# Two matmuls with a GELU between them: the loads, the start and the order of the first blocks rearranged

## The chip, the cores and the metric

One core of one Trainium2 chip. The metric is the device time of one execution in microseconds (us), the median of several executions. All times here are of undisturbed (fast) executions with a mean granted TensorE clock of 0.986 to 1.000 (the share of its full clock that the profile's records show). In the profile TensorE is PE (its weight loads PEld), ScalarE is ACT, VectorE is DVE, GpSimd is POOL and SyncE, which here issues loads and stores, is SP. "The span" is the stretch that the profile of one execution covers; the device time of that execution is some 1.7 us longer.

## The reference

```python
# x: 16 x 512 x 768, w1: 768 x 3072, b1: 3072, w2: 3072 x 768, all float32
y = np.matmul(x, w1) + b1
y = 0.5 * y * (1.0 + erf(y / np.sqrt(2.0)))
return np.matmul(y, w2).astype(np.float32)
```

The kernel works on 16 blocks of 512 rows. For each it computes layer 1 (x times w1, with GELU as y times sigmoid(1.702 y)) and layer 2 (times w2), in bf16 with float32 sums. Layer 1 goes through 24 output chunks of 128 columns (`hc` in the code), six matmuls each. The weights, 9.4 MB each, are loaded once, cast to bf16, and stay on the core.

## The kernel before

x arrives in rows and has to stand in columns, so each block is cast and turned by 24 transposes of 128x128 on TensorE, into PSUM and from there by copies into `xT`. A scheduler decides the order of the instructions on each engine from the order of the code and the times it assumes; only what stands under `manual_schedule` keeps the written order.

```python
w1st = ...tile_pool(name="w1st", bufs=12)     # 128 x 384 float32 each
w2st = ...tile_pool(name="w2st", bufs=4)      # 128 x 768
xfp  = ...tile_pool(name="xfp", bufs=4)       # 128 x 768
gtp  = ...tile_pool(name="gtp", bufs=1)       # layer 1's result of one block
ps_x = ...tile_pool(name="ps_x", bufs=1, space=PSUM)    # the transposes' only target

def stage_w1_group(g):                        # 384 of 3072 columns, six loads of 192 KB
    for kc in range(KC):
        w1s = w1st.tile([P, WG], FP32, name="w1s")
        nc.sync.dma_start(out=w1s[:], in_=w1[kc * P:(kc + 1) * P, c0:c0 + WG])
        # ... cast into w1b: DVE for even kc, ACT for odd

def stage_w2(hc):                             # 128 of 3072 rows, 384 KB, on ACT's DMA queue
    w2s = w2st.tile([P, N], FP32, name="w2s")
    nc.scalar.dma_start(out=w2s[:], in_=w2[hc * P:(hc + 1) * P, :])
    # ... cast into w2b: ACT for odd hc, DVE or GpSimd for even

xbfs0 = load_x_block(0, fast=True)            # four loads of 384 KB, a cast each
# ... bias load, identity
stage_w1_group(0)
xT_cur = transpose_x_block(xbfs0)             # 4 x 6 transposes through ps_x
for _g in range(1, NG):
    stage_w1_group(_g)
xbfs_next = load_x_block(1, fast=True)

for mb in range(n_mblk):
    gT = gtp.tile([P, HC, MB], BF16, name="gT")
    for hc in range(HC):                      # layer 1: 24 x 6 matmuls of 512 columns
        # ... matmuls of w1b and xT_cur into py; ACT: sig = sigmoid(1.702 py + b1s)
        # ... DVE: gT[:, hc, :] = (py + b1t) * sig
        if mb == 0:
            stage_w2(hc)
    if mb == 0:
        # ... layer 2 of block 0: three outputs side by side, in the order w2 arrives;
        # ... six transposes of block 1 after every sixth hc of the first half
    else:
        # ... layer 2: one output after another, 24 matmuls of 384 columns each;
        # ... six transposes of the next block after every second output
```

## Time and profile before

| | before |
|---|---|
| median of 16 runs | 1062.99 us (1060.54 to 1066.15) |
| span of the profiled run | 1058.8 us |
| TensorE busy | 97% |
| first big matmul | 20.70 us |
| first full layer 1 of block 1 begins | 102.42 us |
| one block in steady state | 63.62 us |

### The profile page before, as it was taken

What the parts mean: (1) busy time and instruction counts of PE and PEld (TensorE: products, weight loads), DVE (VectorE), ACT (ScalarE), POOL (GpSimd) and SP (SyncE); (2) the same over time, 40 slices, a digit from 0 to 9 for tenths busy, and PEclk for the clock granted to TensorE, in tenths of its full rate; (3) what the DMA queues carried; (4) which work ended last, traced back from release to release, by engine and by line L of the source; (5) the groups of instructions that cost most, each with busy time, mean ns of one, the idle gap of its engine ahead of it and who ended that gap; (6) DMA issues with size and microseconds to landing.
All of it is one profiled execution on the core that took longest, in us unless ns stands there. A gap on an engine that the chain in (4) does not pass through costs nothing.

```text
span 1058.8 us, 13724 instructions
## 1 busy us (share of the span) xinstructions
PE 1027.2 (97%) x5760; PEld 549.1 (52%) x5760; DVE 357.6 (34%) x527; ACT 355.7 (34%) x537; POOL 30.1 (3%) x41
## 2 busy tenths in 40 slices
PE   3789999999999999999999999999999999999998
PEld 1335464554645555465554645555465554645545
DVE  2531514325142341514325142341514315142340
ACT  4652513324142341513324142341513324142240
POOL 0021000000000000000000000000000000000000
PEclk9999999999999999999999999999999999999999
DMA  9974021120201102021120201102021010100001
GB/s 291 332 278 171 1 83 38 38 83 1 98 24 60 61 23 97 1 82 38 39 82 1 94 26 61 60 23 98 1 82 38 20 41 1 45 15 31 31 8 53
DMA packets 41167, 70.12 MB, mean 66 GB/s; under 512 B 7312, under 2 KB 29840, under 8 KB 41104
## 3 DMA queue, kind: packets, MB, share of 16 engines
q1 hardware_dynamic: 37648, 59.80, 16.8%
q10 hardware_dynamic: 3456, 9.44, 2.5%
q8 instruction: 45, 0.74, 0.3%
q14 instruction: 18, 0.15, 0.0%
HBM read 44.05 MB, written 25.17 MB: 65 GB/s over the span
## 4 chain that ended last, share of the span: by engine, by line
PE 92%; DMA 6%; SPq 1%; ACT 0%; DVE 0%; issue 0%; ACTq 0%
PE po L222 44%; PE py L147 44%; DMA w2s<-in_w_dram 3%; DMA w1s<-in_w_dram 2%; PE pxt L102 2%; PE po L196 1%; SPq L70 1%; PE po L209 1%; DMA xf<-in_x_dram 1%; ACT sig L155 0%; DVE gT L162 0%; ACT w1b L75 0%; ACT w2b L136 0%; DVE w1b L73 0%; DVE xbf L86 0%
## 5 line engine op out<-in xcount | busy, mean ns | idle before, releaser
L147 PE MATMUL py<-xT,w1b 128*128 128x512 bf16 x2304 | 506.3, 382 | 6.1 <-DVE gT L162 5.1
L222 PE MATMUL po<-w2b,gT 128*128 128x384 bf16 x2880 | 479.7, 326 | 0.0
L162 DVE SCALAR_TENSOR_TENSOR gT<-py,b1t,sig 128x512 bf16<-128x512 f32 x384 | 287.9, 751 | 294.9 <-ACT sig L155 294.9
L222 PEld LDWEIGHTS <-gT 128*128 128x128 bf16 x2880 | 279.2, 98 | 180.8
L147 PEld LDWEIGHTS <-w1b 128*128 128x128 bf16 x2304 | 226.1, 98 | 279.3 <-issue 10.4
L155 ACT ACTIVATE sig<-py,b1s 128x512 bf16<-128x512 f32 x384 | 263.1, 687 | 221.0 <-PE py L147 221.0
L182 DVE COPY osb<-po 128x384 f32<-128x384 f32 x64 | 35.5, 558 | 367.4 <-PE po L222 364.3
L184 ACT COPY osb<-po 128x384 f32<-128x384 f32 x64 | 30.4, 479 | 293.8 <-PE po L222 275.9
L108 ACT COPY xT<-pxt 128x768 bf16<-128x768 bf16 x32 | 25.5, 798 | 103.5 <-PE pxt L102 103.5
L102 PE MATMUL pxt<-ident,xbf 128*128 128x128 bf16 x384 | 33.2, 225 | 18.3 <-ACT xT L108 9.8
L95 POOL CAST xbf<-xf 128x768 bf16<-128x768 f32 x28 | 23.4, 838 | 760.2 <-PE pxt L102 756.1
L102 PEld LDWEIGHTS <-xbf 128*128 128x128 bf16 x384 | 27.5, 100 | 27.7 <-issue 10.9
L196 PE MATMUL po<-w2b,gT 128*128 128x384 bf16 x144 | 27.0, 330 | 3.7 <-ACT w2b L136 2.6
L93 ACT CAST xbf<-xf 128x768 bf16<-128x768 f32 x14 | 11.6, 831 | 45.1 <-PE pxt L102 45.1
L196 PEld LDWEIGHTS <-gT 128*128 128x128 bf16 x144 | 14.2, 99 | 14.8 <-issue 5.3
L110 DVE COPY xT<-pxt 128x768 bf16<-128x768 bf16 x32 | 17.6, 549 | 0.6 <-PE pxt L102 0.6
L75 ACT CAST w1b<-w1s 128x384 bf16<-128x384 f32 x24 | 12.3, 511 | 11.3 <-DMA w1s<-in_w_dram 11.2
L136 ACT CAST w2b<-w2s 128x768 bf16<-128x768 f32 x12 | 10.0, 830 | 14.4 <-DMA w2s<-in_w_dram 14.4
L73 DVE CAST w1b<-w1s 128x384 bf16<-128x384 f32 x24 | 8.6, 357 | 15.0 <-DMA w1s<-in_w_dram 15.0
L91 DVE CAST xbf<-xf 128x768 bf16<-128x768 f32 x14 | 8.1, 581 | 2.6 <-DMA xf<-in_x_dram 2.6
L209 PE MATMUL po<-w2b,gT 128*128 128x384 bf16 x48 | 8.3, 326 | 0.0
L134 POOL CAST w2b<-w2s 128x768 bf16<-128x768 f32 x7 | 6.0, 859 | 71.9 <-DMA w2s<-in_w_dram 71.9
(13 smaller groups left out, 16.7 us busy)
## 6 DMA issues: line engine op xcount, KB each, us to landing
xf<-in_x_dram SPq DMA_DIRECT2D x64, 384.0 KB, 3.2
out_dram<-osb SPq DMA_DIRECT2D x128, 192.0 KB, 1.9
w2s<-in_w_dram ACTq DMA_DIRECT2D x24, 384.0 KB, 5.3
w1s<-in_w_dram SPq DMA_DIRECT2D x48, 192.0 KB, 4.4
b1t<-in_b_dram SPq DMA_DIRECT2D x1, 12.0 KB, 7.6
```

The costliest lines, as they stand in the source:

```text
L95: nc.gpsimd.tensor_copy(out=xbf[:], in_=xf32[:])
L102: nc.tensor.transpose(out=pxt[:, kc, :], in_=xbfs[i][:, kc * P:(kc + 1) * P], identity=ident[:],)
L108: nc.scalar.copy(out=dst, in_=pxt[:, :, :])
L110: nc.vector.tensor_copy(out=dst, in_=pxt[:, :, :])
L147: nc.tensor.matmul(out=py[:], lhsT=w1b[:, kc, hc * P:(hc + 1) * P], rhs=xT_cur[:, kc, :], start=(kc == 0), stop=(kc == KC - 1),)
L155: nc.scalar.activation(out=sig[:], in_=py[:], func=mybir.ActivationFunctionType.Sigmoid, bias=b1s[:, hc:hc + 1], scale=1.702,)
L162: nc.vector.scalar_tensor_tensor(out=gT[:, hc, :], in0=py[:], scalar=b1t[:, hc:hc + 1], in1=sig[:], op0=mybir.AluOpType.add, op1=mybir.Alu ...
L182: nc.vector.tensor_copy(out=osb[:], in_=po[:])
L184: nc.scalar.copy(out=osb[:], in_=po[:])
L196: nc.tensor.matmul(out=pos[i][:], lhsT=gT[:, hc, i * P:(i + 1) * P], rhs=w2b[:, hc, nb * NB:(nb + 1) * NB], start=(hc == 0), stop=(hc == H ...
L209: nc.tensor.matmul(out=po3[:], lhsT=gT[:, hc, 3 * P:4 * P], rhs=w2b[:, hc, nb * NB:(nb + 1) * NB], start=(hc == 0), stop=(hc == HC - 1),)
L222: nc.tensor.matmul(out=po[:], lhsT=gT[:, hc, i * P:(i + 1) * P], rhs=w2b[:, hc, nb * NB:(nb + 1) * NB], start=(hc == 0), stop=(hc == HC - 1),)
```

## The change

Its intent: begin layer 1 sooner, leave the DMA to x and w1 first, and let w2 arrive behind layer 1 of two blocks. It has five parts: larger loads on one queue (SP's), three staging buffers for both weights; a start in fixed order with four PSUM targets for the transposes; layer 1 of blocks 0 and 1 before any layer 2 (which needs two `gT`); in steady state single transposes between the matmuls of layer 2; one store per 128 rows instead of two.

```diff
-    w1st = ctx.enter_context(tc.tile_pool(name="w1st", bufs=12))
-    w2st = ctx.enter_context(tc.tile_pool(name="w2st", bufs=4))
-    xfp = ctx.enter_context(tc.tile_pool(name="xfp", bufs=4))
+    wst = ctx.enter_context(tc.tile_pool(name="wst", bufs=3))
+    xfp = ctx.enter_context(tc.tile_pool(name="xfp", bufs=1))
-    gtp = ctx.enter_context(tc.tile_pool(name="gtp", bufs=1))
-    sigp = ctx.enter_context(tc.tile_pool(name="sigp", bufs=4))
+    gtp = ctx.enter_context(tc.tile_pool(name="gtp", bufs=2))
+    sigp = ctx.enter_context(tc.tile_pool(name="sigp", bufs=2))
 ...
+    def stage_w1_cols(c0, n):
+        w1s = wst.tile([P, KC, WG], FP32, name="ws")
+        nc.sync.dma_start(out=w1s[:, :, 0:n], in_=w1r[:, :, c0:c0 + n])
+        # ... six casts
+    def stage_w2_group(wg):
+        w2s = wst.tile([P, 3, N], FP32, name="ws")
+        nc.sync.dma_start(out=w2s[:], in_=w2r[:, 3 * wg:3 * wg + 3, :])
+        # ... three casts
 ...
+    with tc.manual_schedule(engines={PE, Activation, DVE, SP}):       # names shortened
+        xbfs0 = load_x_block(0, fast=True)
+        xT_cur = xtp.tile([P, KC, MB], BF16, name="xT")
+        for i in range(nsub):
+            pxt0 = (ps_o.tile(..., name="po") if i < 3 else ps_x.tile(..., name="pxt"))
+            for kc in range(KC):
+                transpose_x_kc(xbfs0, xT_cur, i, kc, pxt0)
+        stage_w1_cols(0, P)
+        stage_w1_cols(P, WG - P)
+        # ... bias load and b1s
     for _g in range(1, NG):
         stage_w1_group(_g)
     xbfs_next = load_x_block(1, fast=True)
 ...
-            if mb == 0:
-                stage_w2(hc)
+            if mb == 0 and hc % 3 == 0:
+                stage_w2_group(hc // 3)
 ...
+                for hc in range(HC):                   # layer 2, every block
+                    # ... matmul
+                    if pxt is not None and hc % 4 == 0:
+                        transpose_x_kc(xbfs_t, xT_t, i, hc // 4, pxt)
 ...
+    with tc.manual_schedule(engines={PE}):
+        layer1(0, xT_cur, gTs[0])
+        for i in range(nsub):
+            pxt1 = ps_o.tile(..., name="po")
+            for kc in range(KC):
+                transpose_x_kc(xbfs_next, xT1, i, kc, pxt1)
+        gTs[1] = new_gT()
+        layer1(1, xT1, gTs[1])
+        xb = {2: load_x_block(2), 3: load_x_block(3)}
+        xTs = {2: new_xT()}
+        layer2(0, gTs[0], xb[2], xTs[2])
+    # ... layer 2 of block 1, then layer 1 and 2 of each block, transposes two blocks ahead
```

The whole diff also moves x's loads to one of 1.57 MB per block.

## The prediction

> **What bounds the kernel now.** I read the page first (busy shares, slices), then the chain of waits for the rhythm of one block, then a table of windows for the start, then the timeline there.
>
> ```profile
> span 1058.8 us, 13724 instructions
> PE 1027.2 (97%) x5760; PEld 549.1 (52%) x5760; DVE 357.6 (34%) x527; ACT 355.7 (34%) x537; POOL 30.1 (3%) x41
> ...
> DMA  9974021120201102021120201102021010100001
> ```
>
> TensorE is the bound; only the first four of 40 slices have loaded DMA engines. The chain of waits shows a block of 512 rows in steady state (start, length, what):
>
> ```profile
> 165.93 31.08 PE py L147 x144
> 197.01 3.90 PE po L222 x24
> ...
> 201.25 7.80 PE po L222 x48
> ```
>
> Layer 1 of a block takes 31.08 us (144 x 216 ns), layer 2 31.2 us (192 x 162.5 ns), its 24 transposes 24 x 55.6 ns = 1.33 us: 63.6 us, without a gap. Sixteen blocks make 16 x 63.6 = 1018 us. The span is 1058.8, so 41 us are lost, and nothing in the steady part can be won. The windows show where (busy us and counts of PE, PEld, DVE, ACT, POOL, then clock, DMA share, GB/s):
>
> ```profile
> 0.00:20.70 20.70, 3.23 (x25) 2.57 (x26) 5.15 (x12) 8.48 (x13) 0.70 (x6) 1.00 0.90 288
> 20.70:26.52 5.82, 5.82 (x15) 2.01 (x15) 2.18 (x5) 3.39 (x5) 0.00 (x0) 1.00 0.92 304
> 26.52:64.00 37.48, 31.07 (x145) 14.17 (x144) 17.34 (x35) 20.47 (x36) 1.88 (x2) 0.95 0.98 340
> 64.00:102.42 38.42, 34.19 (x206) 19.08 (x204) 10.47 (x16) 14.53 (x22) 7.65 (x9) 1.00 0.59 202
> 165.93:229.55 63.62, 63.62 (x362) 34.21 (x360) 21.65 (x31) 20.83 (x31) 1.65 (x2) 1.00 0.15 50
> ```
>
> The last row is a full block. Layer 1 of block 1 only starts in earnest at 102.42, where 64.9 us of TensorE work (62.3 for block 0, 2.7 for two sets of transposes) has been done: 37.5 us are lost there, the rest at the end. The causes: first big matmul at 20.7; 15 matmuls in the next 5.8 us, so about 427 ns each, half speed; then layer 2 of block 0 in the order of w2's arrival, with waits. The timeline of the start has the events that I rescale:
>
> ```profile
> 4.88 0.56 DVE L86 CAST xbf<-xf 128x768 bf16<-128x768 f32 x1 [4.88 <-DMA xf<-in_x_dram]
> 5.50 0.82 PE L102 MATMUL pxt<-ident,xbf 128*128 128x128 bf16 x6 [5.50 <-DVE xbf L86]
> 14.15 0.79 ACT L108 COPY xT<-pxt 128x768 bf16<-128x768 bf16 x1
> 20.70 18.81 PE L147 MATMUL py<-xT,w1b 128*128 128x512 bf16 x72 [0.97 <-DVE xT L110]
> ```
>
> x arrives at once, but the transposes share one PSUM buffer, and their copies queue in ACT behind casts and their loads: 15 us from first transpose to first matmul. The DMA rates, from a finer table of the same view:
>
> ```profile
> 6.00:7.00 1.00, 0.32 (x4) 0.06 (x1) 0.00 (x0) 0.00 (x0) 0.00 (x0) 1.00 1.04 409
> 10.00:12.00 2.00, 0.00 (x0) 0.00 (x0) 0.09 (x1) 0.70 (x1) 0.00 (x0) 1.00 1.06 46
> 30.00:35.00 5.00, 5.00 (x24) 2.23 (x23) 4.36 (x10) 5.00 (x10) 0.00 (x0) 1.00 1.01 332
> ```
>
> x and w2 (3,072-byte rows) come at about 405 GB/s, w1 (1,536-byte rows, some w2 beside it) at about 330; from 10 to 12 us the engines are full and move almost nothing: that is the bias, 3,072 pieces of 4 bytes, worth 2 us of all DMA.
>
> **What the Trainium skill says.** "TensorE: Matmul & The Clock Gate", Part 1: the array starts at half clock and gets the full one after a busy window of about 3.4 us on a free-running grid; an idle window takes it back. The trace agrees: 427 ns a matmul until 26.5, 216 ns after, and again slow matmuls near 54 us after a thin stretch. Part 4 of that page says that transposes do not count as busy; no number here isolates that. "DMA: Bandwidth & Descriptors", "Why small descriptors are slow": a fixed cost per packet. The two rates above agree: per engine (16) 121 ns for 3,072 bytes and 74 ns for 1,536, so about 28 ns fixed. The same page, "Measured", asks for transfers of 1 MiB or more; but the old small loads already kept the engines 90 to 100% busy, so I credit bigger ones with no rate.
>
> **The change, part by part.** The order of the built instructions on each engine shows four things. (a) SP issues x block 0 as one load, then w1 columns 0-127, 128-383, bias, the other w1 groups, x block 1, then w2; w2 no longer competes from the first microsecond. (b) The four transposes of block 0 get four PSUM buffers and stand first on ACT and DVE. (c) TensorE does layer 1 of blocks 0 and 1 before any layer 2, so w2 has 31 us more to come. (d) In steady state transposes stand singly between matmuls of layer 2, gT has two buffers, stores are 384 KB. (d) is worth nothing: six transposes in a row take 0.33 us, 48 matmuls beside them 7.80, so a switch already costs nothing visible.
>
> The new start:
> 1. x is 1.57 MB. DMA moved its first 1.57 MB by 6.3 us before (adding the windows up), landing is seen about 0.8 later: 7.1. Four casts (DVE 0.56, ACT 0.83): last at 8.8. 24 transposes at half clock (107 ns) end at about 10.4, last copy 11.0, first w1 cast 0.2 after that: first matmul at 11.3, instead of 20.7.
> 2. w1 by then: columns 0-127 in 512-byte rows, 0.39 MB, estimated at 44 ns a packet = 2.1 us, landed 9.2. Columns 128-383 (0.79 MB, 1,024-byte rows, 2.8 us): 12. Bias 2 us: 14. Group 1 (1.18 MB at 330 GB/s = 3.6 us): 17.6, then one group every 3.6 us. TensorE eats a group (3 x 1.295) in 3.9, so it is fed after a small stall, about 0.5 us, before the fourth output chunk. ACT per group needs 3 x 0.69 + 3 x 0.51 = 3.6 us, DVE 3.3: tight, under 3.9.
> 3. Half clock at the start: 12 matmuls x 0.21 = 2.5 us. Layer 1 of block 0 ends at 11.3 + 31.1 + 2.5 + 0.5 = 45.4.
> 4. x block 1 lands behind w1 at about 43 and w2's first group at 45.8. In ACT's order a cast of that w2 group (0.83) and the last sigmoid stand before the two copies of x block 1's transposes (0.8 each), and the fourth transpose set waits for the first one's buffer: copies end at about 49.2. Without this wait the transposes would end at 46.8, so 2.4 us are lost, and the thin stretch of 3.8 us can bring half clock back for one window (1.7 us): I charge 1.0. Layer 1 of block 1 ends at 49.3 + 31.1 + 1.0 = 81.4.
> 5. w2: eight groups of 1.18 MB at 405 GB/s, 2.9 us each: the last at 66, cast 3 or 4 us later, before 81.4. Layer 2 of block 0 then never waits.
>
> At 81.4 TensorE has done as much as at 102.42 before: two layer 1 for one of each, equal within 0.1 us. What remains was 952.9 us (last matmul ends at 1055.3) and is 14 x 31.08 + 16 x 31.2 + 14 x 1.33 = 953.0. The last store doubles: +0.5. Gain = 102.4 - 81.4 - 0.6 = 20.4 us: span 1038.4. The profiled execution took 1.7 us more than its span and was the fastest of six (median 2.6 above). A quieter start should scatter less; I add 1 us: 1041.
>
> **Rivals.**
> - DMA feeds layer 1 too slowly: three staging buffers for everything. For: ACT is nearly full there, and a buffer is free only after its casts. Against: two loads are always queued by my times. If a third of each load's latency showed, 6 to 8 us would be lost: 1048.
> - Single transposes between matmuls each cost a weight load that is not hidden (PEld's mean is 98 ns, a transpose takes 56): 336 x 40 ns = 13 us, 1054. Against: transposes in a row run at 56 ns with a weight load each.
> - x blocks 2 to 4 have one staging buffer, and their casts stand in ACT and DVE before output copies: TensorE would wait for PSUM in the first layer 2. By my times x block 4 lands about 96, just before it is needed; a slip costs 1 to 2 us.
> - The clock stays full through the hand-over and w1 comes at 360 GB/s: 1037.
>
> **Range and chances.** Terms: start +-1, clock +-1.7, feed 0 to 4, scatter +-1: 1036 to 1047. Two per cent of 1063.16 is 21.3 us, that is 1041.9, and my estimate lies on it. Scatter of the old runs favours faster, forgotten waits the other side: 0.53 faster, 0.46 same, 0.01 slower.
>
> **What would show it.** Right: first big matmul near 11.3, the second layer 1 beginning near 49 with ACT's copies as the releaser, the first layer 2 near 81 with no wait on w2, blocks of 63.6 us. Wrong: waits of TensorE on w1 casts of several us, gaps inside layer 2, or blocks longer than 63.7.

## More of the kernel before

The profiled run was the fastest of the 16; a difference of spans is therefore smaller than a difference of medians. The page, the chain, the windows and the start are shown and read in the prediction. Beside them, this is the table of what TensorE waited for (tile and line that waited, who released it, us in total, times, longest us):

```profile
PE pxt L102 <- ACT xT L108: 9.8, 3, 8.7
PE pxt L102 <- DVE xbf L86: 7.0, 2, 5.5
PE py L147 <- DVE gT L162: 5.1, 6, 2.6
PE po L196 <- ACT w2b L136: 2.6, 3, 1.3
```

The first two are the start: copies by ACT that free the transposes' only PSUM buffer, and the x load. The third is layer 1 of block 0 held up by its own GELU, the fourth is layer 2 of block 0 held up by casts of w2. Such waits lie within the first 102 us. Two lines of the timeline there show how the scheduler had mixed the two layers of block 0, six matmuls of layer 1 and then some of layer 2:

```profile
45.02 1.46 PE L147 MATMUL py<-xT,w1b 128*128 128x512 bf16 x6 [0.53 <-DVE gT L162]
46.31 1.30 PE L196 MATMUL po<-w2b,gT 128*128 128x384 bf16 x7
```

## The result, and the profile after

| | before | after |
|---|---|---|
| median | 1062.99 us (16 runs, 1060.54 to 1066.15) | 1037.67 us (8 runs, 1037.44 to 1038.33) |
| ratio, 95% interval | | 0.9762, 0.9751 to 0.9774 |
| span of the profiled run | 1058.8 us | 1036.5 us |
| mean granted clock | 0.998 | 1.000 |

The change is faster by 2.4%. Ratios here and below are the mean time of one kernel's fast runs over that of the other's of the same rounds, so not quite the ratio of the medians quoted. The spans differ by 22.3 us and the medians by 25.3: the profiled run of before was 2.4 us below its median, that of after (1038.25) 0.6 above.

The page of after, its first lines and the line of the DMA in 40 slices:

```profile
span 1036.5 us, 13434 instructions
...
PE 1022.5 (99%) x5760; PEld 548.8 (53%) x5760; DVE 360.0 (35%) x535; ACT 351.8 (34%) x537; POOL 28.6 (3%) x39
...
DMA  9964220110202002030020201202010010100001
```

TensorE has the same 5760 instructions and 4.7 us less busy time (fewer matmuls below full clock); its idle time fell from 31.6 to 14.0 us. What it still waited for, whole:

```profile
PE po L117 <- DVE xbf L103: 7.9, 1, 7.9
PE py L152 <- ACT w1b L77: 0.8, 1, 0.8
PE po L117 <- DVE xT L126: 0.8, 1, 0.8
PE py L152 <- ACT w2b L91: 0.7, 1, 0.7
```

No wait for `gT` is left, and none of layer 2 for w2. (The last line is the start of layer 1 of block 1, which needs no w2: the view names what ended last, and DVE's copy of `xT`, which this layer does need, ended at 48.24, within 0.1 us of its start.) The stages, as a table of windows (columns as in the prediction):

```profile
0.00:11.41 11.41, 2.74 (x24) 2.48 (x25) 2.33 (x7) 4.95 (x9) 0.70 (x6) 1.00 0.90 242
11.41:45.20 33.79, 33.79 (x144) 14.76 (x145) 23.49 (x51) 27.73 (x53) 0.00 (x0) 1.00 1.03 371
45.20:48.29 3.09, 1.67 (x25) 1.37 (x24) 3.09 (x7) 3.09 (x6) 0.00 (x0) 1.00 0.90 300
48.29:79.54 31.25, 31.25 (x145) 14.17 (x146) 21.97 (x32) 20.85 (x31) 6.05 (x7) 1.00 0.71 261
...
144.63:208.25 63.62, 63.62 (x361) 34.18 (x360) 21.71 (x31) 20.83 (x31) 1.65 (x2) 1.00 0.14 50
```

Row by row: the start; layer 1 of block 0; the hand-over (block 1's transposes); layer 1 of block 1; and a steady block, 63.62 us to the hundredth as before. The last column says what the DMA did: 371 GB/s while w1 came, 261 while w2 came beside a TensorE without gaps.

The sum closes. At 79.54 us TensorE has done the work that before had done at 102.42: a gain of 22.9 us. From there to the end before took 956.4 us and after 957.0, so 0.6 is given back, and 22.9 - 0.6 is the 22.3 of the spans. How the 22.9 came about: time lost against full-speed work until then was 37.5 us in before (worked out in the prediction). In after it is 11.41 - 1.33 = 10.1 in the start (1.33 being the transposes at full clock), 33.79 - 31.08 = 2.7 in layer 1, 3.09 - 1.33 = 1.8 in the hand-over and 31.25 - 31.08 = 0.2 in the second layer 1, together 14.7 (14.72 before rounding). So 9.3 us of the gain are the earlier first matmul (20.70 to 11.41), and 13.6 lie in the work behind it. There before had 10.6 us of idle TensorE (37.48 - 31.07 and 38.42 - 34.19 in the prediction's windows), in waits for `gT`, w2 and block 1's x, and by the same windows an estimated 5 us of slow matmuls, besides the slow ones at the start, which after has too.

The timeline of after, first TensorE at the start, then all engines at the hand-over (start, length, engine, line, what; in brackets the idle time before and its releaser):

```profile
7.88 2.10 PE L117 MATMUL po<-ident,xbf 128*128 128x128 bf16 x18 [7.88 <-DVE xbf L103]
...
11.41 3.17 PE L152 MATMUL py<-xT,w1b 128*128 128x512 bf16 x7 [0.79 <-ACT w1b L77]
...
44.71 0.84 ACT L91 CAST w2b<-ws 128x768 bf16<-128x768 f32 x1
...
45.20 1.17 PE L117 MATMUL po<-ident,xbf 128*128 128x128 bf16 x18
...
45.61 1.02 DVE L93 CAST w2b<-ws 128x768 bf16<-128x768 f32 x2
46.01 1.51 ACT L124 COPY xT<-po 128x768 bf16<-128x768 bf16 x2
...
47.14 0.49 PE L117 MATMUL po<-ident,xbf 128*128 128x128 bf16 x6 [0.77 <-DVE xT L126]
...
48.29 31.25 PE L152 MATMUL py<-xT,w1b 128*128 128x512 bf16 x144 [0.65 <-ACT w2b L91]
```

The 24 transposes at the start go without a gap now, where before each set waited for a copy. At 11.41 the matmuls are slow: 7 in 3.17 us. The clock column of the windows reads 1.00 there all the same, so a cold start is seen in the length of the matmuls and not in that column. At the hand-over one w2 cast on ACT and two on DVE stand before copies of block 1's transposes, as the prediction said.

### The profile page after: what moved, and what is told of

It reads as the page before. It is cut to its first block, busy times and chain, and to the rows that moved or that the text cites. A ratio compares the mean times of both kernels' runs of the same rounds, so it can differ in the third digit from the quotient of the medians.

```text
span 1036.5 us, 13434 instructions
## 1 busy us (share of the span) xinstructions
PE 1022.5 (99%) x5760; PEld 548.8 (53%) x5760; DVE 360.0 (35%) x535; ACT 351.8 (34%) x537; POOL 28.6 (3%) x39
## 4 chain that ended last, share of the span: by engine, by line
PE 98%; DMA 1%; ACT 1%; DVE 0%; issue 0%
PE po L187 48%; PE py L152 48%; PE pxt L117 2%; DMA xfs<-in_x_dram 1%; PE po L117 0%; ACT xT L124 0%; DVE gT L167 0%; ACT xbf L105 0%; DVE w2b L93 0%; ACT sig L160 0%; ACT w2b L91 0%; ACT w1b L77 0%; DVE xbf L103 0%; ACT osb L199 0%
## 5 line engine op out<-in xcount | busy, mean ns | idle before, releaser
L187 PEld LDWEIGHTS <-gT 128*128 128x128 bf16 x3072 | 286.3, 98 | 178.0
L117 PE MATMUL pxt<-ident,xbf 128*128 128x128 bf16 x342 | 74.6, 221 | 0.0
L117 PEld LDWEIGHTS <-xbf 128*128 128x128 bf16 x384 | 36.8, 101 | 31.4 <-DVE xbf L103 7.9
L124 ACT COPY xT<-pxt 128x768 bf16<-128x768 bf16 x28 | 22.3, 798 | 85.7 <-PE pxt L117 85.7
L112 POOL CAST xbf<-xfs 128x768 bf16<-128x768 f32 x28 | 23.4, 840 | 686.8 <-PE pxt L117 671.8
L110 ACT CAST xbf<-xfs 128x768 bf16<-128x768 f32 x14 | 11.6, 831 | 43.6 <-PE pxt L117 35.9
L108 DVE CAST xbf<-xfs 128x768 bf16<-128x768 f32 x14 | 7.8, 559 | 40.3 <-PE pxt L117 29.8
L77 ACT CAST w1b<-ws 128x384 bf16<-128x384 f32 (+2 forms) x27 | 10.9, 473 | 0.6 <-DMA ws<-in_w_dram 0.6
L91 ACT CAST w2b<-ws 128x768 bf16<-128x768 f32 x9 | 7.4, 835 | 0.0
L75 DVE CAST w1b<-ws 128x384 bf16<-128x384 f32 (+2 forms) x27 | 7.3, 331 | 0.0
L93 DVE CAST w2b<-ws 128x768 bf16<-128x768 f32 x10 | 6.5, 665 | 0.0
L105 ACT CAST xbf<-xfs 128x768 bf16<-128x768 f32 x4 | 3.1, 828 | 5.2 <-DMA xfs<-in_x_dram 5.2
(12 smaller groups left out, 10.5 us busy)
```

What stands on the lines that cost most here:

```text
L77: nc.scalar.copy(out=dst, in_=w1s[:, kc, 0:n])
L110: nc.scalar.copy(out=xbf[:], in_=xfs[:, i, :])
L112: nc.gpsimd.tensor_copy(out=xbf[:], in_=xfs[:, i, :])
L117: nc.tensor.transpose(out=pxt[:, kc, :], in_=xbfs[i][:, kc * P:(kc + 1) * P], identity=ident[:],)
L124: nc.scalar.copy(out=dst, in_=pxt[:, :, :])
L187: nc.tensor.matmul(out=po[:], lhsT=gT[:, hc, i * P:(i + 1) * P], rhs=w2b[:, hc, nb * NB:(nb + 1) * NB], start=(hc == 0), stop=(hc == HC - 1),)
```

## The experiments

The question after such a result is which part did it, and whether the parts can be had alone. Three groups: undo one part, do one part on the kernel before, and attack what is left. All twelve gave right results. after itself was not run again in their rounds, which were on three different chips, and before's median in them was 1063.34 (u1, u2, u3, u5), 1063.96 (u4, b1, h1, w1) and 1062.56 us (b2, w2, n1, n2). A difference from after of about 1.5 us or less is therefore not shown by the medians alone; the traces have to support it.

| run | median (range), us | ratio to before, 95% |
|---|---|---|
| u1 block by block | 1054.29 (1054.02 to 1055.21) | 0.9922 (0.9898 to 0.9946) |
| u2 old loads | 1074.83 (1073.81 to 1075.65) | 1.0112 (1.0091 to 1.0133) |
| u3 old start | 1044.77 (1044.18 to 1045.22) | 0.9829 (0.9809 to 0.9849) |
| u4 transposes in rows | 1037.97 (1037.58 to 1038.19) | 0.9753 (0.9739 to 0.9768) |
| u5 small loads, one queue | 1041.75 (1041.14 to 1044.54) | 0.9806 (0.9782 to 0.9830) |
| b1 order alone | 1078.53 (1077.40 to 1081.91) | 1.0140 (1.0118 to 1.0162) |
| b2 order, w2 off ACT | 1062.61 (1060.50 to 1064.43) | 0.9996 (0.9984 to 1.0007) |
| h1 hand-over | 1037.42 (1036.93 to 1037.94) | 0.9748 (0.9732 to 0.9765) |
| w1 warm clock | 1046.19 (1045.63 to 1046.36) | 0.9830 (0.9815 to 0.9845) |
| w2 warm clock, same order | 1039.00 (1037.63 to 1039.25) | 0.9769 (0.9745 to 0.9793) |
| n1 no warm-up | 1036.00 (1034.95 to 1036.78) | 0.9743 (0.9722 to 0.9764) |
| n2 all | 1034.88 (1034.64 to 1035.07) | 0.9733 (0.9714 to 0.9753) |

### u1: the order of the blocks undone

```diff
         layer1(0, xTs[0], gTs[0])
-        for i in range(nsub):                # ... block 1's transposes
-        layer1(1, xT1, gTs[1])
-        layer2(0, gTs[0], xb[2], xTs[2])
+        xb[2] = load_x_block(2)
+        layer2(0, gTs[0], xb[1], xTs[1])     # with block 1's transposes
+        layer1(1, xTs[1], gTs[1])
```

> The changed kernel with one part undone: layer 2 of block 0 comes before layer 1 of block 1 again (and x is transposed one block ahead, as before). My account: the order is the largest part. Layer 2 of block 0 begins near 45 us, but w2's last group lands only near 65, so its first group of matmuls ends near 65.5, layer 2 near 94, against 79.5 for the second layer 1 in the changed kernel: 14 to 15 us lost, about 1052. Rival (the gain comes from the loads and the start, the order is a detail): within 4 us of the changed kernel's 1037.7.

Measured: 1054.29, that is 16.6 us more than after. TensorE's waits in it:

```profile
PE po L187 <- ACT w2b L91: 6.6, 3, 2.7
PE po L187 <- DVE w2b L93: 5.6, 5, 1.6
```

Layer 2 of block 0 asks for w2 while it still arrives. 12.2 us of waits are listed; the rest goes with a mean clock of 0.991 against 1.000: matmuls were slower in these thin stretches. The expected time (about 1052) holds, and the rival (the order is a detail) falls. That the order is the largest part does not hold: undoing the loads, which comes next, costs more.

### u2 and u5: the loads undone

u2 brings back the small loads and puts w2 back on ACT's queue:

```diff
-    wst = ctx.enter_context(tc.tile_pool(name="wst", bufs=3))
-    xfp = ctx.enter_context(tc.tile_pool(name="xfp", bufs=1))
+    w1st = ctx.enter_context(tc.tile_pool(name="w1st", bufs=12))
+    w2st = ctx.enter_context(tc.tile_pool(name="w2st", bufs=4))
+    xfp = ctx.enter_context(tc.tile_pool(name="xfp", bufs=4))
 ...            # w1: six loads a group, x: four a block, w2: three a group:
-        w2s = wst.tile([P, 3, N], FP32, name="ws")
-        nc.sync.dma_start(out=w2s[:], in_=w2r[:, 3 * wg:3 * wg + 3, :])
+            w2s = w2st.tile([P, N], FP32, name="w2s")
+            nc.scalar.dma_start(out=w2s[:], in_=w2[hc * P:(hc + 1) * P, :])
```

> The changed kernel with the old loads: 192 and 384 KB each, w2 on ACT's queue from the first microsecond, beside x and w1. My account: w2's first four tiles delay x to about 11 us and later share the DMA engines with w1, whose last columns are cast near 48 instead of 38; layer 1 of block 0 is then fed too slowly and ends near 52 instead of 45: 6 to 8 us lost, about 1045. Rival (with the new order w2 beside w1 hurts nobody): under 2 us lost.

u5 is the same with `nc.sync.dma_start` for w2, so that only the size of the loads is undone and their order stays after's:

```diff
-            nc.scalar.dma_start(out=w2s[:], in_=w2[hc * P:(hc + 1) * P, :])
+            nc.sync.dma_start(out=w2s[:], in_=w2[hc * P:(hc + 1) * P, :])
```

> The changed kernel with small loads (192 and 384 KB, as before) but in the new order on SP's one queue: size alone undone. My account: size is worth nothing; w1 may come at 330 instead of 380 GB/s, but that is hidden, and x in four loads even starts the casts earlier: 1036.5 to 1038.5. Rival (transfers of more than a MiB are what speeds up the start): 4 us or more lost, with first matmuls waiting for w1.

Both missed. u2 came to 1074.83: 30 us above what was expected, and slower than the kernel before. u5 came to 1041.75, 4.1 above after, where the account gave size no worth; its rival, 4 us or more with first matmuls waiting for w1, is what came.

u2 first. TensorE's longest waits in it and ACT at 65 us:

```profile
PE py L153 <- DVE gT L168: 16.8, 6, 5.6
```

```profile
65.55 0.83 ACT L92 CAST w2b<-w2s 128x768 bf16<-128x768 f32 x1 [3.08 <-DMA w2s<-in_w_dram]
...
66.28 1.26 ACT L161 ACTIVATE sig<-py,b1s 128x512 bf16<-128x512 f32 x2
```

This is layer 1 of block 0, which needs no w2. But ACT had a w2 cast in front of it, the cast waited 3.08 us for its load, and the sigmoids behind it waited too (the first had its input from about 62.6, halfway through TensorE's 12 matmuls of 59.99 to 65.27); without sigmoids no `gT`, no free PSUM, no matmul. A cast that waits for data nobody needs yet holds up what stands behind it. Between u2 and u5 lie 33 us, and only w2's queue was edited (the scheduler may then place its casts differently).

Most of u5's loss arises at the start. What SP did from 2.6 us, what it waited for up to 20 us, and the windows from 8 to 10 and 20 to 25 us:

```profile
2.59 8.56 SPq L73 DMA_DIRECT2D w1s<-in_w_dram  x12
```

```profile
SPq L73 <- DMA xfs<-in_x_dram: 3.2, 2, 2.5
```

```profile
8.00:10.00 2.00, 1.00 (x8) 0.74 (x9) 0.99 (x2) 1.07 (x2) 0.00 (x0) 1.00 0.34 103
20.00:25.00 5.00, 4.73 (x15) 1.68 (x15) 2.71 (x6) 2.69 (x5) 0.00 (x0) 0.66 1.05 365
```

Twelve small loads took SP 8.56 us to issue, 3.2 us of it in waiting for loads of x to land; from 8 to 10 us the DMA engines were busy to 34% and moved 103 GB/s (after: 339). From 20 to 30 us it ran at 365 and 370, hardly below after's 373 (from 30 to 35 at 331 against 377, but there TensorE waited for nothing), so it is less the rate of small loads that costs than a start with too few bytes under way. Group 1 of w1 was cast late, three waits of 1.36, 0.34 and 0.27 us fell together with a clock of 0.66, and layer 1 of block 0 ended at 48.79, 3.6 us later than after's. (u5's profiled run was its slowest, 1044.54; the others lay at 1041.1 to 1042.2. Its span is 6.3 us above after's: 3.8 by the start of the second layer 1, at 52.13, and 2.5 within that layer, where ACT again held sigmoids behind w2 casts that waited for their loads, 2.83 us at 73.61. Whether the faster runs had this second part is not known.)

### u3: the start undone

```diff
-    with tc.manual_schedule(engines={PE, Activation, DVE, SP}):       # names shortened
-        xbfs0 = load_x_block(0, fast=True)
-        # ... transposes into four PSUM buffers; w1 columns 0-127, 128-383; bias
+    xbfs0 = load_x_block(0, fast=True)
+    # ... bias
+    stage_w1_group(0)
+    xT_cur = xtp.tile([P, KC, MB], BF16, name="xT")
+    for i in range(nsub):
+        pxt0 = ps_x.tile([P, KC, P], BF16, space=PSUM, name="pxt")     # one buffer, as before
```

> The changed kernel with the old start: one PSUM buffer for the transposes of block 0, the bias ahead of w1, the scheduler's order on ACT and DVE. My account: transposes and copies alternate and stand behind w1 casts, so the first big matmul comes near 16.5 instead of 11.4; nothing later makes up for it: 5 us lost, 1043. Rival (TensorE waits for w1 soon after anyway, so an early start is eaten up): 1 to 2 us lost.

Measured: 1044.77, 7.1 us above after. TensorE in it:

```profile
17.29 32.29 PE L148 MATMUL py<-xT,w1b 128*128 128x512 bf16 x144 [0.65 <-DVE xT L126]
...
53.20 3.25 PE L148 MATMUL py<-xT,w1b 128*128 128x512 bf16 x8 [1.10 <-ACT xT L124]
```

The first big matmul is 5.9 us later than after's; layer 1 then runs 1.7 us shorter. Its hand-over, from 49.41 to 53.20, took 3.8 us instead of 3.1, and behind it 8 matmuls took 3.25 us: here the clock did fall, which in after it did not (144 in 31.25). The first 24 took 7.03 us, 1.85 more than at 216 ns. 5.9 - 1.7 + 0.7 + 1.85 makes 6.75, against 6.5 between the spans. The expectation (1043, first big matmul near 16.5) holds in the main; it left out the clock.

### u4: the single transposes undone

```diff
-                    if pxt is not None and hc % 4 == 0:
-                        transpose_x_kc(xbfs_t, xT_t, i, hc // 4, pxt)
+                if pxt is not None:                    # six in a row behind the 24 matmuls
+                    for kc in range(KC):
+                        transpose_x_kc(xbfs_t, xT_t, i, kc, pxt)
```

> The changed kernel with the transposes six in a row again, after the first half of each row tile's layer 2, instead of singly between matmuls. My account: a switch costs nothing, blocks stay at 63.62 us: within 0.5 us of 1037.7. Rival (single transposes leave a weight load uncovered): 5 us or more gained.

Measured: 1037.97, and blocks of 63.6 us in its chain (layer 1 begins at 143.96 and again at 207.58). One by one or in rows makes no difference, so the rival of 13 us falls.

### b1 and b2: the order alone, on the kernel before

```diff
-    gtp = ctx.enter_context(tc.tile_pool(name="gtp", bufs=1))
+    gtp = ctx.enter_context(tc.tile_pool(name="gtp", bufs=2))
 ...
+    with tc.manual_schedule(engines={PE}):
+        layer1(0, xT_cur, g0)
+        xT1 = transpose_x_block(xbfs_next)
+        layer1(1, xT1, g1)
+        # ... loads of blocks 2 and 3
+        layer2(0, g0, xb[2], xTs[2])
+    # ... then as in after; loads, start and stores as in before
```

> The kernel before with one part of the change: layer 1 of blocks 0 and 1 ahead of any layer 2 (and a second gT buffer), loads and start as before. My account: first big matmul still near 20.7, w1 comes until 48, layer 1 of block 0 ends near 52, block 1's near 90, where the kernel before was at the same amount of work at 102.4: 12 to 13 us gained, 1050. Rival (order is all): 20 us or more gained, 1043 or less. Rival (order is worth nothing without the loads): within 3 us of 1063.

Measured: 1078.53, 15.5 us slower than before; 1050 was expected. The order that is worth 16.6 us on top of the new loads costs 15.5 without them. The window of layer 1 of block 0, and ACT in it:

```profile
21.06:79.14 58.08, 41.68 (x144) 16.05 (x144) 24.17 (x45) 29.57 (x50) 4.13 (x5) 0.85 0.86 293
```

```profile
68.98 0.83 ACT L136 CAST w2b<-w2s 128x768 bf16<-128x768 f32 x1 [5.47 <-DMA w2s<-in_w_dram]
...
69.72 1.26 ACT L152 ACTIVATE sig<-py,b1s 128x512 bf16<-128x512 f32 x2
72.21 0.83 ACT L136 CAST w2b<-w2s 128x768 bf16<-128x768 f32 x1 [1.23 <-DMA w2s<-in_w_dram]
```

Layer 1 took 58 us for 31 us of work: 16.4 us of waits for `gT`, and the rest matmuls below full speed (granted clock 0.85). Between two w2 casts, each waiting for its load, stand two sigmoids: layer 1 goes at the pace of w2. The transposes of block 1 then took another 10.5 us, to 89.64. (This was b1's slowest run, 1081.91.) The kernel before had these waits too, and hardly shorter. ACT's waits for w2 in before, then in b1:

```profile
ACT w2b L136 <- DMA w2s<-in_w_dram: 14.4, 9, 3.9
```

```profile
ACT w2b L136 <- DMA w2s<-in_w_dram: 15.0, 8, 5.5
```

But in before TensorE had matmuls of layer 2 to do in between (the two lines of its timeline at 45 us); the new order takes them away. That this is the difference is argued, not tested.

If the casts on ACT are the cause, taking w2 off ACT should cure it. b2 is b1 with:

```diff
-        nc.scalar.dma_start(out=w2s[:], in_=w2[hc * P:(hc + 1) * P, :])
-        # ... casts on GpSimd, ACT and DVE
+        nc.gpsimd.dma_start(out=w2s[:], in_=w2[hc * P:(hc + 1) * P, :])
+        nc.gpsimd.tensor_copy(out=w2b[:, hc, :], in_=w2s[:])
```

> The kernel of the run with the order alone, and w2 loaded from GpSimd's queue and cast by GpSimd only: w2 still shares the DMA engines with x and w1 from the first microsecond, but no w2 cast or w2 load stands in ACT's and DVE's queues any more. Theory H (the order alone lost 15 us because sigmoids stood in ACT's queue behind casts that waited for w2, so layer 1 ran at w2's pace): layer 1 of block 0 ends near 52 instead of 80, the time falls to about 1050. Theory D (it lost because w2 takes DMA bandwidth from w1): still above 1070.

Measured: 1062.61 in twelve runs, between the two numbers. 15.9 us came from w2's loads on ACT and its casts on ACT and DVE, then; layer 1 of block 0 now ends at 64.56 instead of 79.14. The rest fits the other theory, though no run isolates it: w2 still comes from the first microsecond and takes its share of the DMA. This is ACT near the end of layer 1 of block 0:

```profile
58.70 0.83 ACT L88 CAST xbf<-xf 128x768 bf16<-128x768 f32 x1 [2.19 <-DMA xf<-in_x_dram]
```

ACT's last cast of w1 is at 52.69, and block 1's x, which stands behind w1, is still waited for until 58.70 (in after it was being cast at 42). Its start is the old one besides (first big matmul at 23.16). The kernel then equals before: in these runs the order gained only where w2 came behind w1 and x.

### h1: the hand-over

```diff
+            if mb == 0 and hc == HC - 2:
+                transpose_block1()           # ahead of the last output chunk of layer 1
 ...
-            pxt1 = ps_o.tile([P, KC, P], BF16, space=PSUM, name="po")
+            pxt1 = (ps_o.tile(..., name="po") if i < 3 else ps_x.tile(..., name="pxt"))
```

> The changed kernel with x block 1 transposed before the last output chunk of layer 1 of block 0, and its fourth set in a PSUM buffer of its own. If the 1.8 us between the two layer 1 are ACT's copies standing behind a w2 cast and a sigmoid, plus the wait for a buffer, most of it goes: 1.0 to 1.7 us gained, 1036.0 to 1036.7. If it is something else (x block 1 landing late, the clock), under 0.4 us.

Measured: 1037.42, 0.25 us better than after by the medians (0.7 by the spans), where 1 us or more was expected of the hand-over's 1.8. Its timeline says why:

```profile
45.58 1.02 DVE L93 CAST w2b<-ws 128x768 bf16<-128x768 f32 x2
...
47.59 1.68 PE L152 MATMUL py<-xT,w1b 128*128 128x512 bf16 x7 [0.91 <-DVE xT L126]
```

The transposes were earlier (the first at 43.88), yet the scheduler left w2's casts before the copies. Moving TensorE's part alone is not enough.

### w1 and w2: is the half clock at the start worth anything?

13 matmuls at 427 ns cost 2.7 us in after. Useless matmuls on the identity, while TensorE waits for x, should warm the clock:

```diff
+        pw = ps_y.tile([P, MB], FP32, space=PSUM, name="py")
+        def warm(n):
+            for _ in range(n):
+                nc.tensor.matmul(out=pw[:, 0:P], lhsT=ident[:], rhs=ident[:], start=True, stop=True)
+        warm(64)
         ...                                  # x's transposes
+            warm(4 if i < 3 else 14)
```

> The changed kernel with 64 useless matmuls of the identity before x arrives and 26 among the transposes, so that the clock is full when layer 1 begins. Theory 1 (the 13 matmuls at half clock are on the path): they cost 2.7 us and the transposes another 0.7: 1034.4. Theory 2 (w1's second group, landing at 16.8, would have made TensorE wait at its fourth output chunk anyway, at 17.2, where it now begins near 17.9): only 0.7 us gained, 1037.0, with a new wait on the casts of w1 in the place of the slow matmuls.

Measured: 1046.19, which neither theory had. The edit was not one change: the added instructions made the scheduler put casts of w1's second group, which had yet to land, ahead of the last copies of `xT`:

```profile
17.13 0.92 ACT L77 CAST w1b<-ws 128x384 bf16<-128x384 f32 x2 [7.41 <-DMA ws<-in_w_dram]
17.96 0.79 ACT L124 COPY xT<-po 128x768 bf16<-128x768 bf16 x1
```

So layer 1 began at 18.80. The run says nothing on the clock. w2 has the same useless matmuls in a version whose order on ACT, DVE and SP is written by hand and meant to be after's:

```diff
-    for _g in range(1, NG):
-        stage_w1_group(_g)
+    # ... each load an object; its casts placed after a named output chunk on a named engine:
+        for k, (a, d) in enumerate([(0, 0), (3, 2), (6, 5), (8, 8), (11, 10), (14, 13), (16, 16)], 1):
+            at("DVE", 0, d, on(g[k], "DVE"))
+            at("ACT", 0, a, on(g[k], "ACT"))
+    # ... likewise x block 1, w2 and x block 2, all under manual_schedule
```

> The useless matmuls again, now with ACT's, DVE's and SP's order written by hand so that it is instruction for instruction that of the changed kernel (looked up in the built program; the first try had moved casts and a load). Theory 1 (the slow matmuls are on the path): 3.3 us gained, 1034.4. Theory 2 (the second w1 group lands at 16.8, so the fourth output chunk begins at 17.2 at best, now 17.9): 0.7 us gained or, where the clock falls back in the new wait of 3 us, up to 1 us lost: 1036.8 to 1038.7.

Measured: 1039.00, a little above theory 2's range and 1.3 above after. TensorE at the start, and a window behind it:

```profile
10.96 4.06 PE L156 MATMUL py<-xT,w1b 128*128 128x512 bf16 x18
17.16 29.05 PE L156 MATMUL py<-xT,w1b 128*128 128x512 bf16 x126 [2.15 <-DVE w1b L90]
```

```profile
17.16:20.00 2.84, 2.84 (x9) 1.20 (x10) 1.78 (x4) 2.54 (x6) 0.00 (x0) 0.64 1.02 361
```

The first 18 matmuls, all that w1's first three chunks of columns allow, took 4.06 us: full clock. Then TensorE waited 2.15 us for the second group of w1, until 17.16, and behind that wait the granted clock was 0.64, so the gain was given back: layer 1 ended at 46.05, after's at 45.20. After, at half clock, came to that group at about 18 (13 matmuls at 427 ns and 5 at 216 from 11.41), when it had just been cast. The slow matmuls of after are thus nearly free, as long as w1 comes no sooner. (At the hand-over w2's order is not quite after's: on DVE one `gT` stands before both copies of `xT`, and one matmul of layer 2 comes before the second layer 1. The hand-over took 3.06 us against 3.09, so this does not decide the run.)

### n1 and n2: a version from what was learnt

If w1 sets the pace there, it has to come sooner. The bias load moves 12 KB and holds the DMA for 2 us (46 GB/s from 10 to 12 us, in before and after alike; 363 in n1, which loads it otherwise). n1 has the order by hand, the bias loaded as 24 rows of 512 bytes and turned by TensorE, x block 1 loaded before w1's last group, its transposes before the last chunk with copies ahead of w2's casts, and the last store in two halves:

```diff
-        nc.sync.dma_start(
-            out=b1t[:], in_=b1.rearrange("(hc p) -> hc p", p=P).rearrange("hc p -> p hc")
-        )
+        nc.sync.dma_start(out=b1r[:], in_=b1.rearrange("(hc p) -> hc p", p=P))
+        nc.tensor.transpose(out=pb[:, 0:HC], in_=b1r[:], identity=ident32[0:HC, 0:HC])
+        nc.vector.tensor_copy(out=b1t[:], in_=pb[:, 0:HC])
 ...
+        at("DVE", 0, 22, transpose_block1)
+        at("ACT", 0, 23, on(w2g[0], "ACT"))
+        at("DVE", 0, 23, on(w2g[0], "DVE"))
```

> The changed kernel in the hand-written order with the bias loaded as 24 rows and turned on TensorE (2 us of DMA less ahead of w1's second group), x block 1 transposed before the last output chunk with its load's casts earlier, w2's first casts behind its copies, and the last store in two halves; no useless matmuls. By theory 2 the earlier w1 does nothing while the clock is slow: 1.5 us from the hand-over and 0.4 from the store, 1035.8. By theory 1 also 1035.8.

Measured: 1036.00, 1.7 us under after. TensorE at its start had a surprise:

```profile
8.43 2.10 PE L141 MATMUL po<-ident,xbf 128*128 128x128 bf16 x18 [5.70 <-DVE xbf L116]
10.32 0.85 PE L141 MATMUL pxt<-ident,xbf 128*128 128x128 bf16 x6
11.96 4.06 PE L156 MATMUL py<-xT,w1b 128*128 128x512 bf16 x18 [0.79 <-ACT w1b L90]
```

18 matmuls in 4.06 us: the full clock, with nothing but transposes in the three microseconds before. In after the same transposes were followed by matmuls of 427 ns. n1's times scatter over 1.8 us, after's over 0.9. That the clock is warm in some executions and cold in others would fit, but only one execution has a profile, so that is not shown. The 1035.8 expected was thus met partly by luck: it took the clock for slow at this point, and in the profiled execution (1035.24) it was not.

n2 is n1 with the useless matmuls of w1 and w2.

> The same with the useless matmuls, so that clock and w1 are both early. By theory 2 now both pay, since the second w1 group lands near 14.6: layer 1 of block 0 ends near 41.5 instead of 45.2, 1032. By theory 1 the clock gives 3.3 us here as it did without the bias change: 1032.5. If the useless matmuls bring nothing: 1035.8.

Measured: 1034.88 (1034.64 to 1035.07), the best of all: 2.8 us, 0.3%, under after by the medians, and 2.7% faster than before. 1032 was expected. The hand-over is as intended, 24 transposes with TensorE busy throughout in 1.38 us where after took 3.09. The miss lies at the start, where it is again w1. n2's window of the hand-over, and ACT at the second group of w1:

```profile
42.62:44.00 1.38, 1.38 (x26) 1.38 (x25) 1.21 (x2) 1.25 (x3) 0.00 (x0) 1.00 1.05 407
```

```profile
16.12 1.34 ACT L90 CAST w1b<-ws 128x384 bf16<-128x384 f32 x3 [0.68 <-DMA ws<-in_w_dram]
```

The second group is cast at 16.12, only 0.7 us sooner than in after, where a landing near 14.6 was expected. The bias load now stood first and everything behind it came later (transposes from 8.43 in n1 against 7.88 in after; in n2 the useless matmuls put them off to 8.94). That explains some 0.5 us of the 1.5; the rest is open. The first big matmul is at 11.90, no sooner than after's 11.41. Against n1 the useless matmuls gave 1.1 us by the medians and 0.2 by the spans, and a scatter of 0.4 us.

## Why the prediction was right

It said 1041, in a range of 1036 to 1047, with faster a little likelier than not; 1037.67 was measured, faster by 2.4%. On its own terms the verdict was nearly a coin's throw (1041 against a border of 1041.9); that it fell clearly on one side comes from charges that were too high. By its own steps:

1. First big matmul at 11.3: 11.41. The x load was seen at 7.26 (7.1 predicted), the last copy began at 10.66.
2. w1 at 330 GB/s, a stall of 0.5 us: it came at 371 and more, and the second group's casts, at 16.78 and 16.92, were just in time. The rate was mis-sized; it had been taken from a stretch of before in which w2's loads ran beside w1's. The 28 ns per packet fall with it: at the 373 to 377 GB/s at which after loaded w1 in the same 1,536-byte rows, the same sum leaves some 10.
3. 12 matmuls at half clock: 13. (One sum behind this does not come out: 15 matmuls in 5.8 us are 388 ns each. The 427 ns is the distance of before's weight loads there, of which 14 began before 26.5.) Layer 1 ended at 45.20 (45.4 predicted).
4. The hand-over, predicted to end at 49.3 and to cost 1.0 us of clock: it ended at 48.29, with the copies of ACT and DVE behind casts of w2 as described, but faster, and the clock stayed up. The last copy was DVE's (47.68 to 48.24) and not one of ACT's, which were done at 47.5; there the predicted sign failed. The charge for the clock was wrong for a near-miss: u3's hand-over of 3.8 us, the length that the prediction assumed, did bring half clock back and 1.85 us of cost; after's took 3.1 (one profile each; the length alone does not decide it, see the last section). The second layer 1 therefore ended at 79.54 instead of 81.4. These two terms were mis-sized most: 0.8 for the hand-over and 0.8 for the clock.
5. w2 never waited for: no wait on w2 in layer 2.
6. Single transposes and the rest worth nothing, 0.6 lost afterwards: blocks of 63.62 us, 0.6 lost.

The span was thus 1.9 us too long. The other 1.5 of the miss of 3.3: the prediction added 1 us for scatter, which did not come (after's runs lie within 0.9 us), and the profiled run of after was 0.6 above its median.

The rivals: a feed too slow for three staging buffers did not show (0.8 us of waits on w1, in all, at the first matmul); single transposes cost nothing (u4); x blocks 2 to 4 caused no wait; the last rival, full clock through the hand-over and a faster w1, with 1037, is what happened.

What the prediction did not have is how the parts hang together. It treated order, loads and start as a sum. In before's numbers the order alone loses 15.5 us (b1), and with w2 off ACT it is level (b2). Taking one part away from after loses 16.6 for the order, 7.1 for the start, 37.2 for all of the loads (u2), 4.1 for their size alone (u5), 0.3 for the single transposes (inside the noise). And it "credited bigger ones with no rate", which is nearly right of the rate and yet missed the 4 us of u5, most of it because small loads that wait for one another left the DMA idle for two thirds of the time from 8 to 10 us.

Two things stay open: whether the clock at the start of after and n1 changes from run to run, and how much of the 33 us between u2 and u5 is ACT's queue and how much the order in which w2 comes. b2, which took w2 off ACT but left it coming early, puts the first (with DVE's queue) at 15.9 us in the kernel before; no run split it in after.

## What to carry to other kernels

A load that is not needed yet does harm in two ways: it takes DMA time from those that are, and its cast, waiting ahead of other work on its engine, holds that work up; so put late data last on one queue and its casts behind the work they would block. A new order of the matmuls is worth only what the arrival of the data allows, so test it together with the loads (the same order gained 16.6 us with them and lost 15.5 without). Before paying to remove slow matmuls or a wait, see what would be waited for next: a warm clock at the start ran straight into the load of w1.

## What the Trainium skill lacked or had wrong

- "TensorE: Matmul & The Clock Gate", Part 4, says that transposes do not count as TensorE being busy for the clock. n1 had nothing but 24 transposes in the 3.5 us before its first big matmul, and 18 big matmuls then took 4.06 us, full clock. In after 7 took 3.17 us in the same place, so one run is for the page and one against; Part 1's busy window on a free-running grid could give both, which no run here shows.
- The same page, Part 1, gives the window as about 3.4 us. The length of a slow stretch agrees: worked out from the granted clock in w2 (0.98 from 17.16 to 18 us, 0.50 to 21, 0.81 to 22, then 1.00), in u5 (0.54, 0.50, 0.50 and 0.76 from 21 to 25) and in u3 (0.57 from 53.20 to 56, 0.75 to 58), half clock lasted an estimated 3.4 us each time. But a whole idle window was not needed to lose the clock: 2.15 us of waiting did it in w2, and 2.0 us in three pieces in u5. With transposes alone between two layers, 3.1 us (after) and 3.3 us (u5) left it up and 3.8 us (u3, 24 matmuls in 7.03 us behind it) brought it down.
- "DMA: Bandwidth & Descriptors", "Measured", asks for 1 MiB or more per load on account of bandwidth, measured on loads issued from GpSimd. Issued from SP, loads of 192 KB ran at 365 and 370 GB/s from 20 to 30 us (u5) and loads of 1.18 MB at 373 (after). What size was worth here, 4.1 us, came mostly from the number of bytes under way at the start (103 against 339 GB/s from 8 to 10 us).
- The same page, "Rules for kernel authors", says that a strided last dimension becomes one descriptor per element. It does not say what that costs the other loads: the bias, 3,072 pieces of 4 bytes, filled all 16 DMA engines from 10 to 12 us at 46 GB/s; n1, with 24 rows of 512 bytes instead, moved 363 GB/s there.
- No page consulted here puts a number on a cast that waits for a load ahead of other work on an engine. Between b1 and b2, with w2 taken off ACT and DVE, it was 15.9 us.
